# A rotary embedding kernel on one core: two half-width VectorE products joined into one that reads its halves in reversed order

## The chip, the cores and the metric

The kernel runs on one core of a Trainium2 chip. The metric is the device time in microseconds (us). Where several runs exist, the median is given. The kernel before took 317.52 us (3 runs, 317.51 to 317.86). The record calls a run fast if it is not over 1.5% above the fastest run of the same kernel. In the profiles DVE is VectorE, ACT is ScalarE, POOL is GpSimd and SP is SyncE. The Trainium skill, which some passages name, is a set of notes on the chip.

## The reference

```python
# x: (8, 2048, 16, 64) float32; cos, sin: (2048, 32) float32
x1 = x[..., :32]
x2 = x[..., 32:]
out1 = x1 * cos - x2 * sin          # cos, sin broadcast over batch and heads
out2 = x1 * sin + x2 * cos
return np.concatenate([out1, out2], axis=-1)
```

Input and output are 67.1 MB each. There are only a few operations for each element, so the bytes weigh heavily.

## The kernel before

The 2048 positions are spread over 128 partitions, J = 16 positions in each. One batch is a tile of 128 x 16384 elements in f16. GpSimd issues one casting load per batch (f32 to f16) and one casting store per batch (f16 to f32), all on one DMA queue. Only the first two rows of batch 0 and the last two of batch 7 go another way: ScalarE casts them, and SyncE issues their transfers on a second queue. Five tiles are in use at once, so the loads of batches 5 to 7 wait until an earlier store has landed and its tile is free.

```python
    def rotate(xt):
        v = tmp_pool.tile([P, J, H, D], f16)
        sin_b = sin_h.unsqueeze(2).to_broadcast([P, J, H, Dh])
        neg_b = neg_h.unsqueeze(2).to_broadcast([P, J, H, Dh])
        cos_b = cos_h.unsqueeze(2).to_broadcast([P, J, 2 * H, Dh])
        nc.vector.tensor_mul(out=v[:, :, :, 0:Dh], in0=xt[:, :, :, Dh:D], in1=neg_b)   # L67
        nc.vector.tensor_mul(out=v[:, :, :, Dh:D], in0=xt[:, :, :, 0:Dh], in1=sin_b)   # L68
        xw = xt.rearrange("p j h (e d) -> p j (h e) d", d=Dh)
        nc.vector.tensor_mul(out=xw, in0=xw, in1=cos_b)                                # L70
        xa = xt.rearrange("p j h d -> p (j h d)")
        nc.vector.tensor_add(out=xa, in0=xa, in1=v.rearrange("p j h d -> p (j h d)"))  # L72
    ...
    for b in range(B):
        rotate(tiles[b])
        if b < B - 1:
            store(b, tiles[b])
        if b + NBUF < B:
            tiles.append(load(b + NBUF))
    # ... the last batch is stored in three parts: rows 0 to 8, 9 to 13, and 14 and 15
```

The tables of sine, negative sine and cosine are cast to f16 by ScalarE (ACT) once. The cosine and sine transfers share the DMA engines with the first five loads.

## Time and profile before

| kernel before | value | where it is read |
|---|---|---|
| time | 317.52 us, profiled span 315.6 us | runs, head of the page |
| VectorE busy | 209.2 us, 66% | page, part 1 |
| the loads' and stores' queue | 98.0% of the span of 16 engines | page, part 3 |
| HBM traffic | 67.63 + 67.11 MB, 427 GB/s | page, part 3 |
| the two half products | 4.425 + 4.417 us | groups |
| the other two operations | 8.692 us each | groups |

The first fence has lines of the page of the kernel before. Each digit of the second and third lines is the busy share, in tenths, of one of 40 slices of the span.

```profile
DVE 209.2 (66%) x32; ACT 6.8 (2%) x6; POOL 9.4 (3%) x21
...
DVE  0009599999999999999979999990009994000000
...
DMA  9899999999999999999999999999999999999998
...
q0 software_dynamic: 2448, 99.09, 98.0%
...
HBM read 67.63 MB, written 67.11 MB: 427 GB/s over the span
## 4 chain that ended last, share of the span: by engine, by line
issue 25%; DMA 23%; DVE 21%; another core or an unknown queue 13%; POOL 1%; ACT 1%; SPq 0%; POOLq 0%; DVEq 0%; ACTq 0%
```

VectorE has whole slices with nothing to do; the DMA engines have none. The chain of waits nevertheless gives VectorE 21%. The chain follows who released whom. It does not see that a released transfer then stands behind others in a queue, so it must be read together with the DMA row.

The groups of the same page: line, engine, operation, output and inputs, shapes, count | busy us, mean ns of one | idle time before, and what ended it.

```profile
L70 DVE TENSOR_TENSOR xt<-xt,cos_h 128x16384 f16<-128x16384 f16 x8 | 69.5, 8692 | 4.2 <-ACT cos_h L81 3.9
L72 DVE TENSOR_TENSOR xt<-xt,v 128x16384 f16<-128x16384 f16 x8 | 69.5, 8692 | 0.3
L67 DVE TENSOR_TENSOR v<-xt,neg_h 128x8192 f16<-128x8192 f16 x8 | 35.4, 4425 | 50.1 <-DMA xt<-in_x_dram 49.9
L68 DVE TENSOR_TENSOR v<-xt,sin_h 128x8192 f16<-128x8192 f16 x8 | 35.3, 4417 | 0.0
```

Two sizes give a rate and a fixed part: (8692 - 4421) ns / 8192 elements = 0.521 ns per element, which leaves about 150 ns for each instruction.

The timeline of the kernel before (start us, duration us, engine, line, operation; in brackets the idle time before it and its releaser): batch 1, then the last load and the stores behind it.

```profile
53.65 4.42 DVE L67 TENSOR_TENSOR v<-xt,neg_h 128x8192 f16<-128x8192 f16 x1
...
57.99 4.42 DVE L68 TENSOR_TENSOR v<-xt,sin_h 128x8192 f16<-128x8192 f16 x1
62.44 8.69 DVE L70 TENSOR_TENSOR xt<-xt,cos_h 128x16384 f16<-128x16384 f16 x1
71.17 8.69 DVE L72 TENSOR_TENSOR xt<-xt,v 128x16384 f16<-128x16384 f16 x1
79.89 4.43 DVE L67 TENSOR_TENSOR v<-xt,neg_h 128x8192 f16<-128x8192 f16 x1
...
199.10 0.53 POOL L51 DMA_DIRECT2D xt<-in_x_dram  x1 [56.39 <-DMA out_dram<-xt]
...
237.47 4.42 DVE L67 TENSOR_TENSOR v<-xt,neg_h 128x8192 f16<-128x8192 f16 x1 [24.82 <-DMA xt<-in_x_dram]
...
263.97 0.53 POOL L95 DMA_DIRECT2D out_dram<-xt  x1 [50.50 <-DVE xt L72]
```

Three things are to be seen. A rotation takes 26.24 us (53.65 to 79.89), less than the roughly 39 us that one load and one store take in the queue. The last load is released at 199.10 us by a store that landed, not by VectorE. And the stores of batch 7 are issued at 263.97 us, 52 us before the end: the queue still has other work then. The second half product started 4.34 us after the first, although the first lasted 4.42 us; this matters below.

### The profile page before, as it was taken

The numbers are of one execution on the slowest core, as the hardware profiler recorded it, in microseconds if no ns is written. First come the engines' busy times: TensorE is split into PE (matmuls) and PEld (weight loads), VectorE is DVE, ScalarE is ACT, GpSimd is POOL, SyncE is SP. The second block draws the span as 40 slices with busy tenths as digits, with TensorE's granted clock in tenths as the row PEclk, the third lists the DMA queues.
The fourth block names the chain that finished last, engine by engine and source line by source line (L and its number), as shares of the span: only waits on it lengthen the run. The fifth ranks groups of instructions, "written<-read, shape, count | busy, mean of one in ns | idle before, by whom it ended". The sixth has DMA issues, their size and how long they took to land.

```text
span 315.6 us, 126 instructions
## 1 busy us (share of the span) xinstructions
DVE 209.2 (66%) x32; ACT 6.8 (2%) x6; POOL 9.4 (3%) x21
## 2 busy tenths in 40 slices
DVE  0009599999999999999979999990009994000000
ACT  4010000000000000000000000000000002000000
POOL 3000000000000000010000000100000001000000
DMA  9899999999999999999999999999999999999998
GB/s 278 184 261 207 200 249 216 199 199 249 216 199 266 399 424 507 399 332 233 233 199 199 390 407 399 399 532 266 199 224 507 399 399 498 432 399 399 432 424 341
DMA packets 3024, 101.71 MB, mean 322 GB/s; under 512 B 336, under 2 KB 336, under 8 KB 592
## 3 DMA queue, kind: packets, MB, share of 16 engines
q0 software_dynamic: 2448, 99.09, 98.0%
q1 hardware_dynamic: 576, 2.62, 2.2%
HBM read 67.63 MB, written 67.11 MB: 427 GB/s over the span
## 4 chain that ended last, share of the span: by engine, by line
issue 25%; DMA 23%; DVE 21%; another core or an unknown queue 13%; POOL 1%; ACT 1%; SPq 0%; POOLq 0%; DVEq 0%; ACTq 0%
DMA xt<-in_x_dram 12%; DMA cos_f<-in_cos_dram 11%; DVE xt L70 8%; DVE xt L72 8%; DVE v L68 3%; DVE v L67 1%; ACT head L105 1%; POOL out_dram L58 1%; POOL xt L51 0%; ACT cos_h L81 0%; SPq L45 0%; SPq L36 0%; POOLq L58 0%; DVEq L67 0%
## 5 line engine op out<-in xcount | busy, mean ns | idle before, releaser
L70 DVE TENSOR_TENSOR xt<-xt,cos_h 128x16384 f16<-128x16384 f16 x8 | 69.5, 8692 | 4.2 <-ACT cos_h L81 3.9
L72 DVE TENSOR_TENSOR xt<-xt,v 128x16384 f16<-128x16384 f16 x8 | 69.5, 8692 | 0.3
L67 DVE TENSOR_TENSOR v<-xt,neg_h 128x8192 f16<-128x8192 f16 x8 | 35.4, 4425 | 50.1 <-DMA xt<-in_x_dram 49.9
L68 DVE TENSOR_TENSOR v<-xt,sin_h 128x8192 f16<-128x8192 f16 x8 | 35.3, 4417 | 0.0
L51 POOL DMA_DIRECT2D xt<-in_x_dram x8 | 4.4, 560 | 117.1 <-DMA out_dram<-xt 116.3
L105 ACT CAST head<-xt 128x2048 f32<-128x2048 f16 x1 | 1.9, 1897 | 227.6 <-DVE xt L72 227.6
L58 POOL DMA_DIRECT2D out_dram<-xt x7 | 3.7, 535 | 87.8 <-DVE xt L72 87.8
L95 POOL DMA_DIRECT2D out_dram<-xt x1 | 0.5, 531 | 50.5 <-DVE xt L72 50.5
L75 ACT CAST xt<-head 128x2048 f16<-128x2048 f32 x1 | 1.9, 1898 | 3.4 <-DMA head<-in_x_dram 3.4
L75 ACT ACT_TABLE_LOAD x1 | 1.3, 1283 | 0.7 <-PEq L127 0.7
L81 ACT CAST cos_h<-cos_f 128x512 f16<-128x512 f32 x1 | 0.6, 617 | 18.0 <-DMA cos_f<-in_cos_dram 18.0
L79 ACT CAST sin_h<-sin_f 128x512 f16<-128x512 f32 x1 | 0.6, 617 | 9.1 <-DMA sin_f<-in_sin_dram 9.1
L80 ACT ACTIVATE neg_h<-sin_f 128x512 f16<-128x512 f32 x1 | 0.6, 624 | 0.0
L97 POOL DMA_DIRECT2D out_dram<-xt x1 | 0.5, 531 | 0.0
L127 POOL MEMSET const-float32-0.0<- 128x1 f32 x1 | 0.1, 98 | 0.2 <-issue 0.2
L127 POOL MEMSET const-bfloat16-1.0<- 128x1 bf16 x1 | 0.1, 101 | 0.0
L127 POOL MEMSET const-float32-1.0<- 128x1 f32 x1 | 0.1, 98 | 0.0
L127 POOL MEMSET const-uint8-127<- 128x1 uint8 x1 | 0.1, 98 | 0.0
## 6 DMA issues: line engine op xcount, KB each, us to landing
xt<-in_x_dram POOLq DMA_DIRECT2D x7, 4096.0 KB, 41.1
out_dram<-xt POOLq DMA_DIRECT2D x1, 4608.0 KB, 42.3
xt<-in_x_dram POOLq DMA_DIRECT2D x1, 3584.0 KB, 22.2
out_dram<-xt POOLq DMA_DIRECT2D x1, 2560.0 KB, 47.9
head<-in_x_dram SPq DMA_DIRECT2D x1, 1024.0 KB, 4.7
out_dram<-head SPq DMA_DIRECT2D x1, 1024.0 KB, 8.4
sin_f<-in_sin_dram SPq DMA_DIRECT2D x1, 256.0 KB, 15.2
cos_f<-in_cos_dram SPq DMA_DIRECT2D x1, 256.0 KB, 33.9
```

What stands on the lines that cost most here:

```text
L51: nc.gpsimd.dma_start(out=xt[:, j0:J, :, :].rearrange("p j h d -> p (j h d)"), in_=x[b].rearrange("(p j) h d -> p j (h d)", j=J)[:, j0:J, ...
L58: nc.gpsimd.dma_start(out=out[b].rearrange("(p j) h d -> p (j h d)", j=J), in_=xt)
L67: nc.vector.tensor_mul(out=v[:, :, :, 0:Dh], in0=xt[:, :, :, Dh:D], in1=neg_b)
L68: nc.vector.tensor_mul(out=v[:, :, :, Dh:D], in0=xt[:, :, :, 0:Dh], in1=sin_b)
L70: nc.vector.tensor_mul(out=xw, in0=xw, in1=cos_b)
L72: nc.vector.tensor_add(out=xa, in0=xa, in1=v.rearrange("p j h d -> p (j h d)"))
L75: nc.scalar.copy(out=tiles[0][:, 0:JA, :, :].rearrange("p j h d -> p (j h d)"), in_=head.rearrange("p j h d -> p (j h d)"),)
L79: nc.scalar.copy(out=sin_h, in_=sin_f)
L80: nc.scalar.mul(out=neg_h, in_=sin_f, mul=-1.0)
L81: nc.scalar.copy(out=cos_h, in_=cos_f)
L95: gate = nc.gpsimd.dma_start(out=dst, in_=src)
L105: nc.scalar.copy(out=head.rearrange("p j h d -> p (j h d)"), in_=src)
```

## The change

The intent is to do a rotation with three VectorE instructions in place of four. The negative and the positive sine go into one table of full width, and one product reads x with its two halves swapped, by a negative step over the halves. The elements inside a half keep their order.

```diff
-    sin_h = const_pool.tile([P, J, Dh], f16)
-    neg_h = const_pool.tile([P, J, Dh], f16)
+    sin_h = const_pool.tile([P, J, D], f16)
...
-        sin_b = sin_h.unsqueeze(2).to_broadcast([P, J, H, Dh])
-        neg_b = neg_h.unsqueeze(2).to_broadcast([P, J, H, Dh])
+        shape = [P, J, H, 2, Dh]
+        sin_b = sin_h.rearrange("p j (e d) -> p j e d", e=2).unsqueeze(2).to_broadcast(shape)
...
-        nc.vector.tensor_mul(out=v[:, :, :, 0:Dh], in0=xt[:, :, :, Dh:D], in1=neg_b)
-        nc.vector.tensor_mul(out=v[:, :, :, Dh:D], in0=xt[:, :, :, 0:Dh], in1=sin_b)
+        xe = xt.rearrange("p j h (e d) -> p j h e d", e=2)
+        nc.vector.tensor_mul(
+            out=v.rearrange("p j h (e d) -> p j h e d", e=2), in0=xe[:, :, :, ::-1, :], in1=sin_b
+        )
...
-    nc.scalar.copy(out=sin_h, in_=sin_f)
-    nc.scalar.mul(out=neg_h, in_=sin_f, mul=-1.0)
+    nc.scalar.copy(out=sin_h[:, :, Dh:D], in_=sin_f)
+    nc.scalar.mul(out=sin_h[:, :, 0:Dh], in_=sin_f, mul=-1.0)
```

## The prediction

> **What bounds the kernel now.** The DMA engines. The page's row of DMA shares reads 9 in every slice but the first and last; queue q0 alone is 98.0% of the 16 engines' span, and the HBM line gives 427 GB/s over 315.6 us. VectorE is busy for 209.2 us (66%). The chain of waits puts 21% on VectorE, but while those operations run the stretches view shows DMA shares of 0.98 to 1.08, so I read that chain as work done under a full queue.
>
> The slack, from the timeline: transfers of a batch run through one queue about 19.4 us apart (store 0 landed at 121.8 us, store 1 at 141.1). VectorE finishes batch 0 at 53.6 us; its store gets the queue only at about 102. The tightest place is the end. Batch 7's load lands at 237.4 us, VectorE takes 26.3 us, its stores are issued at 264.0. From 264 to 316 us the queue moves 403 GB/s x 52 us = 21.0 MB, of which batch 7 is 8.4 MB; 12.6 MB, or 31 us (an estimate from these numbers), lie ahead of it. Loads 5, 6 and 7 are issued when an earlier store lands, not when VectorE finishes.
>
> **What the change does.** Per batch, two products of 128x8192 (4.425 + 4.417 us, groups of instructions) become one of 128x16384. The other two operations of that size, also all f16, take 8.692 us. From both sizes: 0.52 ns per element plus about 0.15 us fixed. Joining saves one fixed part, 0.15 us per batch, 1.2 us of VectorE time in all. Nothing else moves: POOL, ACT and SP keep their order, dependencies stay, no DMA changes, and the two small ACT operations for the sine table keep their size (0.62 us).
>
> The question is whether the reversed halves keep two elements per cycle. The innermost step stays 1 (runs of 32); the negative step is one level out. The Trainium skill, "VectorE: DVE Perf Modes", section "What auto-detection actually checks", says the mode of two 16-bit elements per cycle is taken if every tensor is 16-bit with step plus or minus 1. Today's products agree: runs of 32 with gaps take 0.52 ns per element. "Vector Engine (DVE) Microarchitecture Reference", section 5.1, lists an operand with a negative step as not measured, so this trace can't decide it. I expect 8.69 us, with 93% confidence.
>
> **On the critical path.** Of the 0.15 us per batch, nothing: each finish comes a little earlier into a full queue.
>
> **Predicted time: 317.5 us, range 316.6 to 318.4.** Faster by over 2%: 1%. Within 2%: 95%. Slower by over 2%: 4%.
>
> **What in the profile would show it.** VectorE x24 in place of x32, busy about 208 us (66%); the new product x8 at about 8692 ns; batch 0 done still at about 53.6 us, because its sum waits for the cosine table (3.9 us today, a bit more afterwards); batch 4 done 0.6 us earlier; loads 5 to 7 issued at unchanged times; batch 7's load landing at about 237.4; DMA share unchanged.
>
> **What would make it wrong.** At one element per cycle the new product would take about 17.2 us (twice the 8.54 us not fixed, plus 0.15), a batch 34.6 us, VectorE about 277 us. Chained from 23.5 us, batch 7 would finish near 301 us, some 6 us after the queue is ready for it at about 295: about 323 to 325 us, 2% slower. The time would also move if DMA throughput depends on what VectorE does, or on the tables' place in memory; I see no sign of either.

## The result and the profile after

The changed kernel took 318.0 us (6 runs, 317.73 to 318.2); the kernel before, on the same occasion, 317.51 us (6 runs, 317.43 to 317.98). The ratio is 1.0011 with a 95% interval of 0.9998 to 1.0024: no change that stands clear of the noise. Ratios in this document are the mean time of one kernel's fast runs over that of the other's fast runs of the same rounds, so they are not quite the ratios of the quoted medians.

The page of the changed kernel, the same lines as before:

```profile
DVE 208.6 (66%) x24; ACT 6.8 (2%) x6; POOL 9.3 (3%) x21
...
DVE  0009899999999999999769999990008994000000
...
DMA  9899999999999999999999999999999999999997
...
q0 software_dynamic: 2448, 99.09, 97.9%
...
HBM read 67.63 MB, written 67.11 MB: 426 GB/s over the span
## 4 chain that ended last, share of the span: by engine, by line
issue 24%; DMA 22%; DVE 22%; another core or an unknown queue 14%; POOL 1%; ACT 1%; SPq 0%; POOLq 0%; DVEq 0%; ACTq 0%
```

Its groups. The joined product is L67; the numbers of the other two lines have moved by one.

```profile
L67 DVE TENSOR_TENSOR v<-xt,sin_h 128x16384 f16<-128x16384 f16 x8 | 69.5, 8693 | 53.6 <-DMA xt<-in_x_dram 53.5
L71 DVE TENSOR_TENSOR xt<-xt,cos_h 128x16384 f16<-128x16384 f16 x8 | 69.5, 8692 | 1.4 <-ACT cos_h L82 1.2
L73 DVE TENSOR_TENSOR xt<-xt,v 128x16384 f16<-128x16384 f16 x8 | 69.5, 8692 | 0.3
```

Its timeline, the same places:

```profile
51.40 8.69 DVE L67 TENSOR_TENSOR v<-xt,sin_h 128x16384 f16<-128x16384 f16 x1
...
60.12 8.69 DVE L71 TENSOR_TENSOR xt<-xt,cos_h 128x16384 f16<-128x16384 f16 x1
68.85 8.69 DVE L73 TENSOR_TENSOR xt<-xt,v 128x16384 f16<-128x16384 f16 x1
77.58 8.69 DVE L67 TENSOR_TENSOR v<-xt,sin_h 128x16384 f16<-128x16384 f16 x1
...
199.42 0.53 POOL L50 DMA_DIRECT2D xt<-in_x_dram  x1 [56.39 <-DMA out_dram<-xt]
...
237.77 8.69 DVE L67 TENSOR_TENSOR v<-xt,sin_h 128x16384 f16<-128x16384 f16 x1 [24.95 <-DMA xt<-in_x_dram]
...
264.21 0.53 POOL L96 DMA_DIRECT2D out_dram<-xt  x1 [50.56 <-DVE xt L73]
```

The joined product runs at the same rate as the other two operations: 8693 ns. VectorE's busy time fell by only 0.6 us, half of what was predicted: the groups give 70.7 us (35.4 + 35.3) for the half products and 69.5 us for the joined one, but the page counts time in which two instructions overlap only once. A rotation now takes 26.18 us (51.40 to 77.58) in place of 26.24. VectorE finished batch 0 more than 2 us earlier (51.4 against 53.6 us), because the cosine table came earlier in this run. The last load was still released at nearly the same moment (199.4 against 199.1 us), and the last stores were issued at nearly the same moment (264.2 against 264.0 us). That early lead therefore went nowhere.

### The profile page after: what moved, and what is told of

Same layout as the page of the kernel before. It is cut to its first block, busy times and chain, and to the rows that moved or that the text cites. A ratio compares the mean times of both kernels' runs of the same rounds, so it can differ in the third digit from the quotient of the medians.

```text
span 316.0 us, 118 instructions
## 1 busy us (share of the span) xinstructions
DVE 208.6 (66%) x24; ACT 6.8 (2%) x6; POOL 9.3 (3%) x21
## 4 chain that ended last, share of the span: by engine, by line
issue 24%; DMA 22%; DVE 22%; another core or an unknown queue 14%; POOL 1%; ACT 1%; SPq 0%; POOLq 0%; DVEq 0%; ACTq 0%
DMA xt<-in_x_dram 12%; DMA cos_f<-in_cos_dram 10%; DVE xt L73 8%; DVE xt L71 8%; DVE v L67 6%; ACT head L106 1%; POOL out_dram L57 1%; POOL xt L50 0%; ACT cos_h L82 0%; SPq L44 0%; SPq L36 0%; POOLq L57 0%; DVEq L67 0%; ACTq L106 0%
## 5 line engine op out<-in xcount | busy, mean ns | idle before, releaser
L67 DVE TENSOR_TENSOR v<-xt,sin_h 128x16384 f16<-128x16384 f16 x8 | 69.5, 8693 | 53.6 <-DMA xt<-in_x_dram 53.5
L71 DVE TENSOR_TENSOR xt<-xt,cos_h 128x16384 f16<-128x16384 f16 x8 | 69.5, 8692 | 1.4 <-ACT cos_h L82 1.2
L73 DVE TENSOR_TENSOR xt<-xt,v 128x16384 f16<-128x16384 f16 x8 | 69.5, 8692 | 0.3
## 6 DMA issues: line engine op xcount, KB each, us to landing
sin_f<-in_sin_dram SPq DMA_DIRECT2D x1, 256.0 KB, 13.2
```

Of the source, the lines that this page charges most:

```text
L67: nc.vector.tensor_mul(out=v.rearrange("p j h (e d) -> p j h e d", e=2), in0=xe[:, :, :, ::-1, :], in1=sin_b)
```

## The experiments

The main theory, D: the DMA queue is full from the first microsecond to the last, VectorE has some 31 us of slack at its tightest place, and so no VectorE change of this size can be seen in the time. The rivals: C, that VectorE's share of the chain of waits is time that a shorter VectorE gives back, so that some loss must have cancelled a gain; P, that the negative step costs rate; S, that the change has a real cost of 0.4 us.

### The changed kernel again, and the table alone

`after_again` is the changed kernel unaltered. `table_only` takes over the merged table and keeps the two half products:

```diff
-        nc.vector.tensor_mul(
-            out=v.rearrange("p j h (e d) -> p j h e d", e=2), in0=xe[:, :, :, ::-1, :], in1=sin_b
-        )
+        sin_p = sin_h[:, :, Dh:D].unsqueeze(2).to_broadcast([P, J, H, Dh])
+        sin_n = sin_h[:, :, 0:Dh].unsqueeze(2).to_broadcast([P, J, H, Dh])
+        nc.vector.tensor_mul(out=v[:, :, :, 0:Dh], in0=xt[:, :, :, Dh:D], in1=sin_n)
+        nc.vector.tensor_mul(out=v[:, :, :, Dh:D], in0=xt[:, :, :, 0:Dh], in1=sin_p)
```

> The changed kernel once more, on another occasion, timed in five rounds against the kernel before. Theory D (the DMA engines bound both kernels; the small difference of 0.4 us in the first comparison is not caused by the shorter VectorE work): within 0.5 us of the kernel before, 317.3 to 318.3 us, of either sign. Rival S (the change costs a real 0.4 us somewhere): again 0.3 to 0.5 us slower than the kernel before, with an interval clear of zero.

> Only the merged signed-sine table is taken over; the two half-size products of the kernel before stay and read its two halves. Theory D: 317.3 to 318.3 us, VectorE x32 again, products about 4.42 us each. Rival S, in the form that the table's layout costs the 0.4 us: as slow as the changed kernel. If the joined product costs it: as fast as the kernel before.

Measured: `after_again` 317.79 us (317.45 to 318.65) against 317.62 us (317.15 to 317.99), ratio 1.0012, interval 0.9999 to 1.0024. `table_only` 317.64 us, ratio 1.0005, interval 0.9992 to 1.0018; its VectorE was busy for 209.2 us in 32 instructions again. Both gave the right result. The difference in medians shrank from 0.5 to 0.2 us, and both of the changed kernel's intervals include no difference, if barely. Rival S is not confirmed, and a real cost of about 0.1% is not excluded by these times: the changed kernel came out that much above on both occasions.

The traces show where the 0.4 us between the two profiled runs arose. The load of batch 0 landed 0.58 us later in the changed kernel (its first product starts at 24.09 against 23.51 us), before VectorE had done anything. Load 5 was released at 122.13 against 121.83 us, and from there to the end both runs took the same 193.8 to 193.9 us, as did `after_again`, `table_only`, `no_product` and `last_plus2`. An early or a late release comes with either kernel: `after_again`, the changed kernel unaltered, released load 5 at 121.86 us (span 315.7 us), and `before_x2`, which has the tables and products of the kernel before, at 122.23 us. `last_plus2` (below), which contains the whole change, was not slower than the kernel before (ratio 0.9991). So the difference of this pair arose in the first 122 us of the DMA queue and not in the shorter VectorE work. What stays open is whether the change makes a late release more frequent; that is too small to matter for the choice.

### Both kernels with VectorE as the bottleneck

To see the size of the saving where it counts, every batch is rotated twice in each of the two kernels (wrong result). VectorE then needs 52 us per batch, more than the queue.

```diff
         rotate(tiles[b])
+        rotate(tiles[b])
```

> The kernel before with every batch rotated twice (wrong result on purpose), so that VectorE needs about 52.5 us per batch, more than the 39 us that the queue needs for its load and store: VectorE should bound it. Expected about 470 to 475 us, VectorE busy about 418 us. It is the partner of the next run. Time from one rotation to the next: 26.25 us, as the timeline of the kernel before has it.

> The changed kernel with every batch rotated twice (wrong result on purpose), VectorE bound. The prediction's size (0.15 us saved per rotation, the difference of the mean durations): about 2.3 us faster than its partner over 15 chained rotations. The rival size, read from the starts in the two timelines (one rotation to the next 26.25 us before, 26.18 us after): only 0.07 us per rotation, 1.0 us in all, because neighbouring operations overlap by part of the fixed time. Rival P (the new product loses rate under load): slower than its partner.

Measured: 469.14 us (4 runs, 469.11 to 469.32) and 468.81 us (6 runs, 468.46 to 471.09). The time is not precise enough, so the traces decide. First the VectorE and DMA rows of the page of `before_x2`: the DMA engines now have empty slices and VectorE has none between its first operation and its last.

```profile
DVE  0089999999999999999999999999999999999910
...
DMA  8989999999699989989488004920088004920088
```

The timelines of `before_x2` and then `after_x2`, the first cosine product and the last sum:

```profile
34.06 8.69 DVE L70 TENSOR_TENSOR xt<-xt,cos_h 128x16384 f16<-128x16384 f16 x1 [1.17 <-ACT cos_h L81]
...
436.49 8.69 DVE L72 TENSOR_TENSOR xt<-xt,v 128x16384 f16<-128x16384 f16 x1
```

```profile
34.04 8.69 DVE L71 TENSOR_TENSOR xt<-xt,cos_h 128x16384 f16<-128x16384 f16 x1 [1.34 <-ACT cos_h L82]
...
435.47 8.69 DVE L73 TENSOR_TENSOR xt<-xt,v 128x16384 f16<-128x16384 f16 x1
```

From the first to the second there are 15 joined products: 402.43 us before, 401.43 us after, a saving of 1.00 us or 0.067 us per rotation. The prediction's 0.15 us would have made 2.25 us. The reason is in the timeline before: the two half products do not depend on each other, and the second begins 4.34 us after the first, 0.08 us before the first one's recorded end. Operations that depend on each other (L68 to L70) begin about 0.03 us after the end of the one before. Half of the "fixed part" of 0.15 us was thus already hidden. Two runs described below support that independence is what counts. In `no_product` the cosine products of batches 0 and 1, which do not depend on each other, take 17.29 us together, 0.09 us less than two of 8.69 us. In `product_twice` the same product is repeated into the same tile, so it must wait, and it starts 8.72 us after the first.

Two places of the Trainium skill bear on this. "Vector Engine (DVE) Microarchitecture Reference", section 5.2, gives about 75 ns per instruction after queue overlap, for streams of 4-byte elements; that is near the 67 ns here. "VectorE: DVE Perf Modes", section "The DRAIN you can't avoid", says that a next operation that is not held starts earlier, and the 4.34 us agree; by held the page does not mean a wait for a result, so the part of independence rests on the traces here.

The end-to-end medians differ by only 0.33 us. In the two profiled runs the first part of batch 7's store took 12.5 us to land before and 13.2 us after, which took back 0.7 of the 1.0 us. There is one profiled run of each, so it stays open whether this is chance.

### VectorE made much shorter

`no_product` leaves out the sine product and the sum (wrong result):

```diff
-        v = tmp_pool.tile([P, J, H, D], f16)
-        nc.vector.tensor_mul(
-            out=v.rearrange("p j h (e d) -> p j h e d", e=2), in0=xe[:, :, :, ::-1, :], in1=sin_b
-        )
...
-        nc.vector.tensor_add(out=xa, in0=xa, in1=v.rearrange("p j h d -> p (j h d)"))
```

> The changed kernel without the sine product and the sum (wrong result on purpose): VectorE busy falls by 139 us to about 70 us. Theory D: 318 us within 1 us, since the transfers are the same and the queue stays full. Rival C (VectorE's 22% of the chain of waits is time that a shorter VectorE gives back): two of three operations gone, some 45 us faster.

Measured: 317.8 us (4 runs), ratio to the kernel before 1.0, interval 0.9975 to 1.0024. From the page of `no_product`, VectorE's busy time, the DMA row and the chain:

```profile
DVE 69.4 (22%) x8; ACT 6.8 (2%) x6; POOL 9.3 (3%) x21
...
DMA  9899999999999999999999999999999999999997
...
issue 24%; DMA 23%; another core or an unknown queue 21%; DVE 8%; POOL 1%; ACT 1%; SPq 0%; DVEq 0%; POOLq 0%; ACTq 0%
```

VectorE's work fell by two thirds, its share of the chain from 22% to 8%, and the time stayed. Its place in the chain went to "another core or an unknown queue": in order of time, that piece begins when a store is issued (78 us in the changed kernel, 55 us here) and ends in both at about 121.9 us, when store 0 has landed and load 5 can go. VectorE's time in the chain had only covered part of that wait. Rival C falls. The HBM line of the page also stayed at 426 GB/s, so the transfers ran no faster beside an idler VectorE.

### VectorE made longer, everywhere and at the tightest place

`product_twice` repeats the joined product in every batch, about the work that a joined product at one element per cycle would have cost. `last_plus2` and `last_plus5` do it three and six times in batch 7 alone. All three give the right result.

```diff
# product_twice: the product stands twice in rotate()
+        nc.vector.tensor_mul(
+            out=v.rearrange("p j h (e d) -> p j h e d", e=2), in0=xe[:, :, :, ::-1, :], in1=sin_b
+        )
# last_plus2 (times=3) and last_plus5 (times=6)
-    def rotate(xt):
+    def rotate(xt, times=1):
+        for _ in range(times):    # around the product
-        rotate(tiles[b])
+        rotate(tiles[b], times=3 if b == B - 1 else 1)
```

> The changed kernel with the sine product done twice per batch (right result), which puts the VectorE work at what it would have been with the new product at one element per cycle: 34.9 us per batch, about 278 us busy. Theory D with the slack of the prediction: batch 7 is done at about 303 us, 8 us after the queue is ready for it at 295, and the last transfers then start into an empty queue: 323 to 328 us. Rival C: VectorE time counts from the start, some 40 us or more slower.

> The changed kernel with the sine product of batch 7 alone done three times (right result): 17.4 us of VectorE work added at the tightest place. Theory D with 31 us of slack there: 318 us within 0.7 us. Rival C: 17 us slower.

> The changed kernel with the sine product of batch 7 alone done six times (right result): 43.6 us added at the same place. Theory D with 31 us of slack: 13 us beyond the slack, and 2 to 3 us for a queue that has run dry, 330 to 335 us. Rival C: 44 us slower, 361 us. No change would mean that the slack is larger than estimated.

| kernel | VectorE work added | time, us (4 runs) | ratio to the kernel before | interval |
|---|---|---|---|---|
| last_plus2 | 17.4 us in batch 7 | 317.4 | 0.9991 | 0.9971 to 1.001 |
| last_plus5 | 43.6 us in batch 7 | 331.28 | 1.0427 | 1.0406 to 1.0448 |
| product_twice | 8.7 us in each batch | 327.36 | 1.03 | 1.0279 to 1.032 |

All three lie where theory D put them. The stretches of `last_plus5` show where the slack ends (window, its length, busy us of VectorE, ACT and POOL with counts, TensorE clock, DMA share, GB/s; over stretches this short a share can come out above 1, so only the zeros are used):

```profile
288.00:290.00 2.00, 1.97 (x2) 0.00 (x0) 0.00 (x0) 1.00 1.07 459
...
293.00:294.00 1.00, 1.00 (x1) 0.00 (x0) 0.00 (x0) 1.00 0.00 0
...
296.00:307.00 11.00, 10.97 (x2) 0.00 (x0) 0.00 (x0) 1.00 0.00 0
307.00:309.00 2.00, 0.11 (x1) 1.79 (x1) 1.05 (x2) 1.00 0.69 295
```

The queue runs dry at about 293 us and stands empty until batch 7's stores are issued at 307.4 us. In the changed kernel those stores are issued at 264.2 us, so the slack is about 29 us. The ends agree with it: 43.6 us were added and the profiled span grew by 13.3 us (316.0 to 329.3), so 30.3 us were absorbed. The prediction's estimate was 31 us.

### One transfer less

`store6_less` leaves batch 6 unstored (its output is wrong). Nothing waits for that store.

```diff
-        if b < B - 1:
+        if b < B - 2:
             store(b, tiles[b])
```

> The changed kernel without the store of batch 6 (its output stays unwritten, wrong on purpose). No load and no VectorE operation waits for that store, and it isn't in the chain of waits. Theory D: one transfer of 8.4 MB less in a full queue, 19.4 us faster, 297.5 to 300 us. Rival C (the chain of waits is the bound): no change, 318 us.

Measured: 297.96 us (4 runs, 297.89 to 298.59) against 317.36 us, ratio 0.9393, interval 0.9375 to 0.9411. The 19.4 us are the 8.4 MB of that store at 432 GB/s (8.39 / 19.4). VectorE does all of its work as before. A transfer that the chain of waits doesn't name is worth its full time in the queue; two thirds of the VectorE work, which the chain does name, are worth nothing.

### How reading order affects the rate

`patterns` gives the product of each batch another reading order of x (wrong result), each on a source line of its own:

```diff
+        if b == 0 or b == 7: in0 = xe[:, :, :, ::-1, :]                                            # L69, halves reversed
+        elif b == 1:         in0 = xe                                                              # L71, plain
+        elif b == 2:         in0 = xt[:, :, :, ::-1]                                               # L74, all 64 backwards
+        elif b == 3:         in0 = xt.rearrange("p j h (d e) -> p j h e d", e=2)                   # L77, innermost step 2
+        else:                in0 = xt.rearrange("p j h (e d) -> p j h e d", d=n)[:, :, :, ::-1, :] # L84, L86, L88: n = 2, 8, 16
```

(Shortened: in the kernel each branch holds the whole product, with the other operands shaped to match.)

> The product of each batch reads x in another order (wrong result on purpose): batches 0 and 7 halves reversed as in the change, 1 in plain order, 2 all 64 elements backwards (innermost step -1), 3 even then odd elements (innermost step 2), 4, 5 and 6 blocks of 2, 8 and 16 in reversed order. Durations of one product: theory D[...]: 8.69 us for all but batch 3, and about 17.2 us for batch 3. Rival P (a negative step or short runs cost rate): batches 2, 4, 5 or 6 longer than 8.69 us, the shorter the run the longer.

The groups of `patterns`:

```profile
L69 DVE TENSOR_TENSOR v<-xt,sin_h 128x16384 f16<-128x16384 f16 x2 | 17.4, 8692 | 43.7 <-DMA xt<-in_x_dram 43.7
L77 DVE TENSOR_TENSOR v<-xt,sin_h 128x16384 f16<-128x16384 f16 x1 | 17.2, 17226 | 0.0
L74 DVE TENSOR_TENSOR v<-xt,sin_h 128x16384 f16<-128x16384 f16 x1 | 8.7, 8693 | 0.0
L84 DVE TENSOR_TENSOR v<-xt,sin_h 128x16384 f16<-128x16384 f16 x1 | 8.7, 8693 | 0.0
L71 DVE TENSOR_TENSOR v<-xt,sin_h 128x16384 f16<-128x16384 f16 x1 | 8.7, 8692 | 0.0
```

Blocks of 8 and 16 (L86, L88) took 8692 ns as well. Only the innermost step of 2 costs: 17226 ns, twice the part that is not fixed. Reversed blocks down to two elements, and an innermost step of -1, cost nothing. Rival P falls. The rule of the Trainium skill ("VectorE: DVE Perf Modes", section "What auto-detection actually checks") that 16-bit tensors with step plus or minus 1 get two elements per cycle agrees with all eight batches. The whole run took 317.17 us with 8.5 us more VectorE work in batch 3; it is one run of unknown state, so its time is not used as evidence. Each order was measured in one or two instructions.

## Why the prediction was right or wrong

- **The time: right.** Predicted 317.5 us (316.6 to 318.4), measured 318.0.
- **What binds: right, and shown.** With 139 us less VectorE work the time stayed at 317.8 us. With one store less and all the VectorE work it fell by 19.4 us.
- **The slack at the end: right.** Estimated 31 us; 17.4 us more work in batch 7 were hidden, and of 43.6 us more, 30.3 us were absorbed.
- **The rate of the joined product: right.** 8693 ns against a forecast of 8.69 us. The part that was open, the negative step, is now measured.
- **The size of the saving: too large by a factor of two.** The step "Joining saves one fixed part, 0.15 us per batch, 1.2 us of VectorE time in all" failed. Measured: 0.067 us per rotation and 0.6 us of busy time. The two half products were independent and overlapped, which adding up their mean durations hides. The starts in the timeline, 4.34 us apart, had shown it already.
- **The cosine wait: wrong in its size.** It was to be a bit more than 3.9 us; it was 1.2 us, because the cosine table landed 2.3 us earlier and the load of batch 0 0.6 us later. This is not the change's doing: the cast of the cosine table began at 35.55 us in the kernel before, at 33.41 us in `before_x2` with its unchanged tables, and at 35.79 us in `store6_less` with the merged one. The same shift moved batch 0's end to 51.4 us, where 53.6 was forecast, and batch 4's end by 2.5 us in place of 0.6. (The prediction also said that batch 0's sum waits for the table; it is the cosine product that does.)
- **What a product at one element per cycle would cost: slightly low.** The prediction said 323 to 325 us. The stand-in with the product done twice took 327.36 us; it carries 34.91 us per batch where the prediction reckoned 34.6, so batch 7 was done at 303.5 us and not near 301, and the queue ran dry at about 293 us, not 295. A kernel with all its products at one element per cycle was not run.

Left open: whether the changed kernel is really slower by 0.1% (1.0011 and 1.0012 on two occasions). In the profiled pair the difference arose in the first 122 us of the DMA queue, where both kernels show early and late cases.

## What to carry to other kernels

Before costing a saving, look at whether the busiest resource has empty slices. If it has none, find the tightest place of the engine to be improved and reckon its slack from the bytes still queued there; the chain of waits alone does not show it. To cost the joining of two independent instructions, take start-to-start times from the timeline, not the sum of durations. A swap of blocks can be folded into the reading order of an f16 product at no cost in the cases measured here: blocks of 2, 8, 16 and 32 in reversed order, and all 64 elements backwards. An innermost step of 2 doubled the part that is not fixed.

## What the Trainium skill lacked or had wrong

- "Vector Engine (DVE) Microarchitecture Reference", section 5.1, lists an operand with a negative step as not measured. Here, with two f16 inputs of 128x16384: halves of 32 reversed 8693 ns, blocks of 16, 8 and 2 reversed 8692 to 8693 ns, innermost step -1 8693 ns, against 8692 ns in plain order. An innermost step of 2 took 17226 ns.
- "DMA: Bandwidth & Descriptors", section "Where 436 GB/s comes from", says without a condition that for transfers between HBM and SBUF the HBM side, about 358 GB/s per core, binds. Here one core moved 427 GB/s of HBM reads and writes over a whole span of 315.6 us. Only the wording of that section is too wide: the same page, section "Measured (HBM→SBUF, 128 partitions, SWDGE, issued from GpSimd)", limits the figure of about 358 to both cores of a pair streaming, and gives 425 GB/s for 16 MB loaded by a core alone, near the 427 here. No run here used a second core.
